# One row as a tile of its own, first in the queue; first weights right behind the memory tokens; small rows on GpSimd's queue

## The chip, the core and the metric

The kernel runs on one core of a Trainium2 chip. The core has TensorE (PE in the profile: matrix products and transposes), VectorE (DVE), ScalarE (ACT), GpSimd (POOL) and SyncE (SP, which only issues transfers here), and 16 DMA engines that serve the transfers that any engine issues. The metric is the device time of one execution in microseconds, the median of several runs.

## The reference

Two layers of a decoder trunk: a norm, one wide projection that feeds four token mixers, an output projection, and a feed-forward block. The fourth mixer attends into 256 memory tokens, and the start of the kernel, where the change lies, prepares it:

```python
def rmsnorm(x, g):
    y = x * lax.rsqrt(jnp.mean(x * x, axis=-1, keepdims=True) + EPS)
    return y * g

mem_n = rmsnorm(mem, mem_norm)                      # (256, 1024)
for l in range(2):
    h = rmsnorm(x, norm_mix[l])                     # (512, 1024)
    mk, mv = jnp.split(mem_n @ mem_w_kv[l], 2, axis=-1)   # 4 heads of 128 each
    mk = rmsnorm(mk.reshape(1, 256, 4, 128), mem_k_norm[l])
    ...
```

Everything is float32. `mem_w_kv[l]` is 1024 x 1024.

## The kernel before

**Products in three parts.** Every float32 product runs as three TensorE passes on split operands: a = a_hi + a_lo, and a·b is a_hi·b_hi + a_hi·b_lo + a_lo·b_hi. `mm3` (L267 to L272) issues the three; in the profile they are lines L270, L271, L272. Splitting an operand takes a ScalarE copy that rounds (w_hi, mt_hi, L97 being the line of the helper `A` that issues every ScalarE operation) and a VectorE subtraction (w_lo at L225, mt_lo at L394).

**Weights.** A `Chunk` (L212) loads 1 MB of weights into `w_raw` (two buffers) over SP's queue and splits it in two halves of 128 x 1024, each with one w_hi and one w_lo (three buffers each). A product needs the half of its rows; for the first weights of the memory, rows 0 to 511 (pieces 0 to 3 of the contraction) are the first half and 512 to 1023 the second.

**The start.** A few constants are set. TensorE runs 14 products on a constant (L143) as a warm-up. The memory tokens `mem_in` (1 MB, 256 x 1024) are loaded over SP's queue (L150), then eight small parameter tensors go into one tile `rows`, one parameter of 128 values per partition (L151 to L157): rows 0 to 39 (two norms and the memory's norm) over ScalarE's queue, rows 40 to 77 (conv_w, hgrn_lower_bounds, hgrn_out_norm, mem_q_norm, mem_k_norm) over SP's. One transpose turns `rows` (78 rows) into `prm`, 128 x 78 (L160, L161), so that each parameter is a column that ScalarE and VectorE can scale with; `g_mem(c)` is the memory norm's column for piece c of 8. GpSimd's queue carries five further loads (two gq_raw, two gk, the positions) and GpSimd makes two masks by a select (causal_bias, tri_f), from which VectorE derives `future` and `tri`.

**Memory tokens.** `mem_in_T` (L388) takes the 8 pieces c: two transposes into a PSUM tile `tr` (three buffers), an mt_hi and an mt_lo. Then two squares of the memory tokens with a sum (ScalarE, tile mem_sq) for the norm. `mem_kv(0)` (L433) has four weight chunks of 256 columns; for each, and for each half of the tokens, 24 products, and behind them copies (ku), squares (mk_sq), a norm and transposes. It runs in alternation with `first_h` (L404), which loads x in two transfers of 1 MB (`xin`), takes four squares of it (also into mem_sq), and transposes and splits it.

**Order.** A scheduler puts the instructions of each engine in one order at build time, by the order of the code and by priority (`high_priority` for the splits of weights); on the chip each engine works them off in that order, and waits on semaphores. A dependency of the kind `order` adds no semaphore, it only fixes two instructions' order on one engine. On SP the order is: memory tokens, five rows, first weights, x, x, second weights, third weights and so on. The changed kernel differs from this one in the order of TensorE's first 800 or so products of some 10,000, and in what goes with them on the other engines.

Of the kernel before, what the change touches and what calls it, by code (L numbers as in the profile page):

```python
# [21 lines left out]
P = 128  # L22
# [47 lines left out]
def hybrid_trunk(ctx: ExitStack, tc: tile.TileContext, x, mem, positions, norm_mix, w_in, conv_w,  # L70
# [38 lines left out]
    def tr_ps():  # L109
        return pat.tile([P, 512], F32, name="tr", bufs=TR_BUFS)  # L110
# [34 lines left out]
    rows = sp.tile([P, P], F32, name="rows")  # L145
    n_rows = 78
    warm = consts.tile([P, 1], F32, name="warm")
    A(warm, one, AF.Exp)
    mem_in = sp.tile([P, 2, D], F32, name="mem_in")
    nc.sync.dma_start(mem_in, mem[0].rearrange("(t p) d -> p t d", p=P))  # L150
    for lo, src in ((0, norm_mix.rearrange("l (c p) -> (l c) p", p=P)),  # L151
                    (16, norm_ffn.rearrange("l (c p) -> (l c) p", p=P)),
                    (32, mem_norm.rearrange("(c p) -> c p", p=P)),
                    (40, conv_w.rearrange("l w (c p) -> (l w c) p", p=P)),
                    (64, hgrn_lower_bounds.rearrange("l (c p) -> (l c) p", p=P)),
                    (72, hgrn_out_norm), (74, mem_q_norm), (76, mem_k_norm)):
        (nc.scalar if lo < 40 else nc.sync).dma_start(rows[lo:lo + src.shape[0], :], src)  # L157
    prm = consts.tile([P, n_rows], F32, name="prm")
    ps = tr_ps()
    pe.transpose(ps[:, :n_rows], rows[:n_rows, :], ident[:n_rows, :n_rows])  # L160
    A(prm, ps[:, :n_rows], AF.Copy)  # L161
# [7 lines left out]
    def g_mem(c):  # L169
        return prm[:, 32 + c:33 + c]  # L170
# [41 lines left out]
    class Chunk:  # L212
        def __init__(self, src, kt, n):
            self.kt, self.step = kt, min(kt, 1024 // n)
            raw = wpool.tile([P, 2048], F32, name="w_raw", bufs=RAW_BUFS)[:, :kt * n].rearrange("p (k n) -> p k n", n=n)
            nc.sync.dma_start(raw, src.rearrange("(k p) n -> p k n", p=P))
            self.parts = []
            for k in range(0, kt, self.step):
                e = min(kt, k + self.step)
                m = (e - k) * n  # L220
                hi, lo = (wpool.tile([P, 1024], F32R, name=nm, bufs=W_BUFS)[:, :m].rearrange("p (k n) -> p k n", n=n)
                          for nm in ("w_hi", "w_lo"))
                with tc.high_priority(offset=AHEAD):
                    A(hi, raw[:, k:e], AF.Copy)
                    dve.tensor_sub(lo, raw[:, k:e], f(hi))  # L225
                self.parts.append((range(k, e), hi, lo))

# [38 lines left out]

    def mm3(ps, a, b, first, last):  # L267
        ah, al = a
        bh, bl = b
        pe.matmul(ps, ah, bh, start=first, stop=False)  # L270
        pe.matmul(ps, ah, bl, start=False, stop=False)  # L271
        pe.matmul(ps, al, bh, start=False, stop=last)  # L272
# [115 lines left out]
    def mem_in_T():  # L388
        for c in range(KD):
            ps = tr_ps()  # L390
            for t in range(2):
                pe.transpose(ps[:, t * P:(t + 1) * P], mem_in[:, t, c * P:(c + 1) * P], ident)
            A(mt[0][:, c, :], ps[:, :MEM], AF.Copy, scale=g_mem(c))
            dve.scalar_tensor_tensor(mt[1][:, c, :], ps[:, :MEM], g_mem(c), f(mt[0][:, c, :]),  # L394
                                     op0=OP.mult, op1=OP.subtract)
        for t in range(2):
            A(mem_sq, mem_in[:, t, :], AF.Square, scale=D ** -0.5, accum_out=mem_ss[:, t:t + 1])
        rstd_into(mem_r, mem_ss, small, 2)
        dve.tensor_copy(mem_r4.rearrange("p (a b) -> p a b", b=2), mem_r[:, :, None].to_broadcast([P, 2, 2]))
        dve.tensor_mul(mem_r2, mem_r4, mem_r4)  # L400

# [31 lines left out]
    def mem_kv(l):  # L433
        kv = sp.tile([P, 4, 2, 2, MEM], F32R, name="kv", bufs=1)
        for q in range(2):
            w = wchunk(mem_w_kv[l][:, q * 256:(q + 1) * 256], KD, 256)
# [38 lines left out]
    mem_in_T()  # L475
# [19 lines left out]
    A(e0, e0, AF.Exp)  # L495
    A(e1, e1, AF.Exp)
# [634 lines left out]
```

## Time and profile before

| | us |
|---|---|
| median of 3 runs (2047.14 to 2047.64) | 2047.41 |
| the profiled execution | 2046.88 |
| its span, first to last instruction | 2044.9 |
| TensorE busy | 2032.3 |
| VectorE busy | 1274.7 |
| ScalarE busy | 1022.0 |
| TensorE's first product with w_lo | 14.03 |
| TensorE's first product of the second weights with w_lo | 22.16 |

The mean granted TensorE clock is 0.999 of full speed. Times within the execution count from the start of its span. In a row of a timeline, the first number is the start, the second the time busy; "out<-in" names the tiles; "x3" says that three instructions are drawn together; brackets give the idle time before it and what ended it. PEld is TensorE's weight load, SPq and ACTq are the parts of SP and ScalarE that issue transfers. In the list of queues, q1 is SP's, q10 ScalarE's, q0 GpSimd's.

### The profile page before, as it was taken

To read this page: it belongs to the slowest core of one execution; us is meant where nothing else is said; L and a number is where in the kernel's file an instruction comes from. 1 tells how busy PE (TensorE), PEld (TensorE's weight loads), DVE (VectorE), ACT (ScalarE), POOL (GpSimd) and SP (SyncE) were. 2 spreads that over 40 slices of the span, in tenths; PEclk is the share of its full clock that TensorE was granted. 3 is DMA by queue.
4 is the path that set the end of the run, shared out by engine and by line. 5 is a ranking of instruction groups with operands and counts; after the bars stand their busy time and mean duration, and the time that the engine had idled before them with its cause. 6 is when DMAs were issued, how large, how long until landed. Compare 5 with 4: busy or idle time off the path is not lost.

```text
span 2044.9 us, 26596 instructions
## 1 busy us (share of the span) xinstructions
PE 2032.3 (99%) x10348; PEld 1714.7 (84%) x10348; DVE 1274.7 (62%) x2519; ACT 1022.0 (50%) x1844; POOL 9.8 (0%) x33
## 2 busy tenths in 40 slices
PE   8999999999999999999999999999999999999999
PEld 8998988888888888888889898888888788888887
DVE  6779998547676544334457889953777654533442
ACT  7653655766665423223355466576766633322231
POOL 0000000000000000000000000000000000000000
PEclk9999999999999999999999999999999999999999
DMA  7623222223233232232243213322222423323222
GB/s 253 219 88 94 68 93 93 64 71 93 83 113 114 87 100 92 93 110 97 88 155 94 88 59 112 93 73 63 83 83 83 144 89 97 103 73 112 93 83 93
DMA packets 187709, 203.79 MB, mean 100 GB/s; under 512 B 4271, under 2 KB 176385, under 8 KB 187457
## 3 DMA queue, kind: packets, MB, share of 16 engines
q1 hardware_dynamic: 183296, 193.04, 29.7%
q10 hardware_dynamic: 4128, 8.93, 1.2%
q8 instruction: 81, 1.33, 0.3%
q14 instruction: 44, 0.35, 0.1%
q0 software_dynamic: 160, 0.13, 0.0%
HBM read 191.60 MB, written 10.49 MB: 99 GB/s over the span
## 4 chain that ended last, share of the span: by engine, by line
PE 98%; DMA 1%; ACT 1%; DVE 1%; issue 0%; SPq 0%; DVEq 0%
PE mm L270 30%; PE mm L271 29%; PE mm L272 29%; PE tr L726 1%; PE tr L720 1%; PE at L697 1%; PE at L696 1%; PE at L272 1%; PE at L270 1%; PE at L271 1%; DMA w_raw<-in_mem_w_kv_dram 1%; PE at L974 0%; PE at L948 0%; PE tr L664 0%; PE tr L765 0%; PE tr L631 0%
## 5 line engine op out<-in xcount | busy, mean ns | idle before, releaser
L270 PE MATMUL mm<-h_hi,w_hi 128*128 128x512 f32 x1664 | 652.0, 393 | 1.0 <-DVE fg L1075 0.4
L225 DVE TENSOR_TENSOR w_lo<-w_raw,w_hi 128x1024 fp32r<-128x1024 f32 (+1 forms) x346 | 419.7, 1214 | 372.3 <-ACT w_hi L97 371.9
L271 PE MATMUL mm<-h_lo,w_hi 128*128 128x512 f32 x1664 | 651.5, 392 | 0.0
L272 PE MATMUL mm<-h_hi,w_lo 128*128 128x512 f32 x1664 | 649.1, 391 | 0.0
L97 ACT ACTIVATE w_hi<-w_raw 128x1024 fp32r<-128x1024 f32 (+1 forms) x346 | 363.3, 1051 | 452.5 <-PE mm L271 406.1
L270 PEld LDWEIGHTS mm<-h_hi,w_hi 128*128 128x128 f32 x1664 | 312.7, 188 | 66.0 <-DVE fg L1075 1.2
L272 PEld LDWEIGHTS mm<-h_hi,w_lo 128*128 128x128 f32 x1664 | 312.6, 188 | 64.2 <-issue 0.2
L271 PEld LDWEIGHTS mm<-h_lo,w_hi 128*128 128x128 f32 x1664 | 312.8, 188 | 63.0 <-issue 1.0
L272 PE MATMUL mm<-w_hi,h_lo 128*128 128x256 f32 (+1 forms) x448 | 128.2, 286 | 0.0
L271 PE MATMUL mm<-w_lo,h_hi 128*128 128x256 f32 (+1 forms) x448 | 127.0, 284 | 0.0
L270 PE MATMUL mm<-w_hi,h_hi 128*128 128x256 f32 (+1 forms) x448 | 127.0, 285 | 0.0
L271 PE MATMUL mm<-a_lo,w_hi 128*128 128x512 f32 x272 | 106.3, 391 | 0.0
L270 PE MATMUL mm<-a_hi,w_hi 128*128 128x512 f32 x272 | 106.0, 390 | 0.0
L272 PE MATMUL mm<-a_hi,w_lo 128*128 128x512 f32 x272 | 105.7, 391 | 0.0
L270 PE MATMUL mm<-y_hi,w_hi 128*128 128x512 f32 x256 | 100.7, 395 | 1.2 <-ACT y_hi L97 1.2
L272 PE MATMUL mm<-y_hi,w_lo 128*128 128x512 f32 x256 | 100.4, 392 | 0.0
L271 PE MATMUL mm<-y_lo,w_hi 128*128 128x512 f32 x256 | 100.3, 392 | 0.0
L272 PEld LDWEIGHTS mm<-w_hi,h_lo 128*128 128x128 f32 x448 | 85.7, 191 | 1.4 <-issue 0.8
L270 PEld LDWEIGHTS mm<-w_hi,h_hi 128*128 128x128 f32 x448 | 85.3, 191 | 1.2 <-issue 0.8
L271 PEld LDWEIGHTS mm<-w_lo,h_hi 128*128 128x128 f32 x448 | 85.6, 191 | 0.6
L97 ACT ACTIVATE a_hi<-fg 128x512 fp32r<-128x512 f32 x44 | 27.8, 633 | 106.8 <-DVE fg L1080 106.8
L97 ACT ACTIVATE prob<-prob,small 128x128 f32<-128x128 f32 (+3 forms) x128 | 69.2, 555 | 15.2 <-DVE small L709 14.6
(370 smaller groups left out, 2958.1 us busy)
## 6 DMA issues: line engine op xcount, KB each, us to landing
w_raw<-in_w_in_dram SPq DMA_DIRECT2D x72, 1024.0 KB, 5.3
w_raw<-in_ffn_w_up_dram SPq DMA_DIRECT2D x44, 1024.0 KB, 5.1
w_raw<-in_w_lift_dram SPq DMA_DIRECT2D x32, 512.0 KB, 3.4
w_raw<-in_ffn_w_down_dram SPq DMA_DIRECT2D x16, 1024.0 KB, 5.4
w_raw<-in_mem_w_kv_dram SPq DMA_DIRECT2D x8, 1024.0 KB, 5.2
w_raw<-in_w_out_dram SPq DMA_DIRECT2D x8, 1024.0 KB, 5.3
w_raw<-in_ffn_w_down_dram SPq DMA_DIRECT2D x10, 512.0 KB, 3.4
kv<-kv ACTq DMA_DIRECT2D x8, 512.0 KB, 6.4
```

The source lines that it names most:

```text
L97: i = act.activation(dst, src, func, **kw)
L225: dve.tensor_sub(lo, raw[:, k:e], f(hi))
L270: pe.matmul(ps, ah, bh, start=first, stop=False)
L271: pe.matmul(ps, ah, bl, start=False, stop=False)
L272: pe.matmul(ps, al, bh, start=False, stop=last)
L696: pe.matmul(ps, q[:, hh, s], k[0][:, :n], start=True, stop=False)
L697: pe.matmul(ps, q[:, hh, s], k[1][:, :n], start=False, stop=True)
L720: pe.transpose(pp[:, (2 * e + i) * P:(2 * e + i + 1) * P], probs[2 * i + e][:, b * P:(b + 1) * P], ident)
L726: pe.matmul(pv[e * HD:(e + 1) * HD, :], vt[:, b, :], pt[:, b, e * 2 * P:(e + 1) * 2 * P], start=b == 0, stop=b == t)
```

## The change

The memory's norm row gets a tile of its own, `mem_row` (8 x 128), loaded by the first transfer of SP's queue, with a transpose and a column tile `mem_g` of its own; rows 32 to 39 of `rows` are set to zero instead. The five other small rows move from SP's queue to GpSimd's. The transpose of `rows` comes after the memory tokens' transposes. The first chunk of weights is made inside `mem_in_T`, ahead of piece 4: its load is next on SP behind the memory tokens; its first half is split ahead of the copies of pieces 4 to 7, its second half behind them. The squares of the memory tokens come after that. Behind the transposes of each piece stands a product on a constant, of which nothing is used. Two exponentials of the lower bounds come after the third w_hi or later.

```diff
     rows = sp.tile([P, P], F32, name="rows")
+    dve.memset(rows[32:40, :], 0.0)
...
+    mem_row = sp.tile([KD, P], F32, name="mem_row")
+    nc.sync.dma_start(mem_row, mem_norm.rearrange("(c p) -> c p", p=P))
     nc.sync.dma_start(mem_in, mem[0].rearrange("(t p) d -> p t d", p=P))
...
-                    (32, mem_norm.rearrange("(c p) -> c p", p=P)),
...
-        (nc.scalar if lo < 40 else nc.sync).dma_start(rows[lo:lo + src.shape[0], :], src)
+        (nc.scalar if lo < 40 else nc.gpsimd).dma_start(rows[lo:lo + src.shape[0], :], src)
+    mem_g = consts.tile([P, KD], F32, name="mem_g")
...
-    ps = tr_ps()
-    pe.transpose(ps[:, :n_rows], rows[:n_rows, :], ident[:n_rows, :n_rows])
-    A(prm, ps[:, :n_rows], AF.Copy)
+    def columns(dst, src, n, since=None):
+        ps = tr_ps()
+        i = pe.transpose(ps[:, :n], src[:n, :], ident[:n, :n])
+        if since is not None:
+            tc.add_manual_dep(i.ins, since.ins.name, order, reason="transposes first")
+        return A(dst, ps[:, :n], AF.Copy)
...
     class Chunk:
-        def __init__(self, src, kt, n):
+        def __init__(self, src, kt, n, held=False):
...
+            self.rest = self.make(raw)
+            for _ in range(1 if held else kt):
+                next(self.rest, None)
+
+        def make(self, raw):
+            kt, n = self.kt, raw.shape[2]
             for k in range(0, kt, self.step):
...
                 with tc.high_priority(offset=AHEAD):
-                    A(hi, raw[:, k:e], AF.Copy)
-                    dve.tensor_sub(lo, raw[:, k:e], f(hi))
+                    splits.append(A(hi, raw[:, k:e], AF.Copy))
+                    low = dve.tensor_sub(lo, raw[:, k:e], f(hi))
+                lowered.append(low)
                 self.parts.append((range(k, e), hi, lo))
+                yield
...
     def mm3(ps, a, b, first, last):
...
-        pe.matmul(ps, ah, bh, start=first, stop=False)
+        i = pe.matmul(ps, ah, bh, start=first, stop=False)
+        if turned:
+            tc.add_manual_dep(i.ins, turned.pop().ins.name, order, reason="transposes first")
...
     def mem_in_T():
+        first = []
+        columns(mem_g, mem_row, KD)
+        idle = at_ps()
+        keep = None
         for c in range(KD):
+            if c == 4:
+                first.append(Chunk(mem_w_kv[0][:, :256], KD, 256, True))
             ps = tr_ps()
             for t in range(2):
-                pe.transpose(ps[:, t * P:(t + 1) * P], mem_in[:, t, c * P:(c + 1) * P], ident)
...
+                i = pe.transpose(ps[:, t * P:(t + 1) * P], mem_in[:, t, c * P:(c + 1) * P], ident)
+                if t == 0 and keep is not None:
+                    tc.add_manual_dep(i.ins, keep.ins.name, order, reason="in between")
+            keep = pe.matmul(idle[:, :P], ones_d, ones_d, start=True, stop=True)
+            tc.add_manual_dep(keep.ins, i.ins.name, order, reason="in between")
+            copies.append(A(mt[0][:, c, :], ps[:, :MEM], AF.Copy, scale=g_mem(c)))
+            lows.append(dve.scalar_tensor_tensor(mt[1][:, c, :], ps[:, :MEM], g_mem(c), f(mt[0][:, c, :]),
+                                                 op0=OP.mult, op1=OP.subtract))
+            if c >= 4:
+                tc.add_manual_dep(copies[c].ins, splits[0].ins.name, order, reason="weights first")
+                tc.add_manual_dep(lows[c].ins, lowered[0].ins.name, order, reason="weights first")
+            if c == 3:
+                turned.append(i)
+        next(first[0].rest)
+        for c in range(4, KD):
+            tc.add_manual_dep(splits[1].ins, copies[c].ins.name, order, reason="copies first")
+            tc.add_manual_dep(lowered[1].ins, lows[c].ins.name, order, reason="copies first")
+        columns(prm, rows, n_rows, i)
         for t in range(2):
-            A(mem_sq, mem_in[:, t, :], AF.Square, scale=D ** -0.5, accum_out=mem_ss[:, t:t + 1])
+            square = A(mem_sq, mem_in[:, t, :], AF.Square, scale=D ** -0.5, accum_out=mem_ss[:, t:t + 1])
+            tc.add_manual_dep(square.ins, splits[1].ins.name, order, reason="copies first")
...
     def mem_kv(l):
...
-            w = wchunk(mem_w_kv[l][:, q * 256:(q + 1) * 256], KD, 256)
+            w = first_chunk.pop() if first_chunk else wchunk(mem_w_kv[l][:, q * 256:(q + 1) * 256], KD, 256)
...
-    mem_in_T()
+    first_chunk = mem_in_T()
     steps(mem_kv(0), first_h())
...
-    A(e0, e0, AF.Exp)
-    A(e1, e1, AF.Exp)
+    for e in (e0, e1):
+        i = A(e, e, AF.Exp)
+        tc.add_manual_dep(i.ins, splits[2].ins.name, order, reason="weights first")
```

More of the change, by code (lines that the diff above doesn't have):

```diff
@@ L169, in g_mem @@
     def g_mem(c):
-        return prm[:, 32 + c:33 + c]
+        return mem_g[:, c:c + 1]
     def g_conv(l, w, c):
@@ L212, in hybrid_trunk @@
     class Chunk:
-        def __init__(self, src, kt, n):
+        def __init__(self, src, kt, n, held=False):
             self.kt, self.step = kt, min(kt, 1024 // n)
             raw = wpool.tile([P, 2048], F32, name="w_raw", bufs=RAW_BUFS)[:, :kt * n].rearrange("p (k n) -> p k n", n=n)
-            nc.sync.dma_start(raw, src.rearrange("(k p) n -> p k n", p=P))
+            loads.append(nc.sync.dma_start(raw, src.rearrange("(k p) n -> p k n", p=P)))
             self.parts = []
+            self.rest = self.make(raw)
[3 more added lines that the diff above has]
+            kt, n = self.kt, raw.shape[2]
             for k in range(0, kt, self.step):
@@ L265, in tokens_wide @@
             k0 += w.kt
+    copies, lows, loads, splits, lowered, turned = [], [], [], [], [], []
     def mm3(ps, a, b, first, last):
@@ L400, in mem_in_T @@
         dve.tensor_mul(mem_r2, mem_r4, mem_r4)
+        return first
     norms = []
```

3 lines of the change are left out of this document (removed).

## The prediction

> **What bounds the kernel now.** First the page: the share of each engine.
>
> ```profile
> span 2044.9 us, 26596 instructions
> ...
> PE 2032.3 (99%) x10348; PEld 1714.7 (84%) x10348; DVE 1274.7 (62%) x2519; ACT 1022.0 (50%) x1844; POOL 9.8 (0%) x33
> ```
>
> TensorE idles 2044.9 - 2032.3 = 12.6 us in all. An edit that adds no matmul of weight can win no more than that, so the next view is the one that says where those 12.6 us lie: the chain of waits over the first 30 us, in order of time (start, length, what).
>
> ```profile
> 0.81 5.30 DMA mem_in<-in_mem_dram
> ...
> 6.40 0.41 SPq L216
> ...
> 7.98 11.79 DMA w_raw<-in_mem_w_kv_dram
> 19.79 1.07 ACT w_hi L97
> 20.88 1.24 DVE w_lo L225
> 22.16 0.39 PE mm L271
> ...
> 24.21 0.12 PE mm L270
> ```
>
> The memory tokens land at 0.81 + 5.30 = 6.11. The queue on SP then issues the first weights (6.40), two halves of x, and the second weights (7.98), which land at 19.77. ScalarE and VectorE split them, and TensorE goes on at 22.16. The last row shows the step from one product to the next, 0.12 us. Everything behind 22.16 is TensorE's own work, so what an edit of the start is worth is how far it moves the 22.16, less what it makes late behind it. Why the weights are issued only at 6.40 is in the waits of SP's queue:
>
> ```profile
> SPq L157 <- DMA mem_in<-in_mem_dram: 3.4, 1, 3.4
> ```
>
> A small row (L157) stands in front of the weights and waits 3.4 us for the memory tokens. How tight the stretches are, and the granted clock, by windows (busy time of each engine, granted clock, DMA share, GB/s):
>
> ```profile
> core 0: us, PE busy (x) PEld busy (x) DVE busy (x) ACT busy (x) POOL busy (x), PEclk, DMA share, GB/s
> 4.40:7.80 3.40, 1.70 (x15) 1.51 (x13) 0.37 (x3) 1.64 (x3) 0.67 (x3) 1.00 0.58 172
> 7.80:11.20 3.40, 2.23 (x13) 1.29 (x13) 2.48 (x13) 2.99 (x12) 0.00 (x0) 1.00 1.03 343
> 11.20:14.60 3.40, 1.57 (x9) 1.07 (x9) 2.48 (x10) 2.94 (x5) 0.00 (x0) 1.00 1.03 411
> 14.60:18.00 3.40, 3.40 (x19) 3.40 (x18) 2.75 (x12) 3.37 (x8) 0.00 (x0) 0.52 1.05 369
> 18.10:30.00 11.90, 11.36 (x95) 11.15 (x94) 6.98 (x14) 10.05 (x29) 0.00 (x0) 1.00 0.72 224
> 30.00:45.00 15.00, 15.00 (x130) 15.00 (x130) 12.87 (x31) 12.35 (x30) 0.00 (x0) 1.00 0.62 212
> 45.00:70.00 25.00, 24.90 (x204) 24.33 (x203) 19.80 (x72) 18.89 (x47) 0.52 (x1) 1.00 0.88 304
> ```
>
> Two things are to be seen. ScalarE works 10.05 of the 11.90 us from 18.10 to 30.00: it has 1.85 us to spare there and no more. And TensorE's clock was granted at half from 14.6 to 18.0, which cost nothing, since TensorE had to wait for the second weights anyway. The timelines give the unit prices (start, busy, engine, line, tiles, count):
>
> ```profile
> 1.12 4.98 PE L144 MATMUL tr<-ones_d 128*128 128x128 f32 x28 [1.12 <-DVE ones_d L118]
> 14.03 0.39 PE L271 MATMUL mm<-w_lo,mt_hi 128*128 128x256 f32 x1 [0.76 <-DVE w_lo L225]
> 15.35 0.41 PE L270 MATMUL mm<-w_hi,mt_hi 128*128 128x256 f32 x1
> 15.56 0.42 PE L271 MATMUL mm<-w_lo,mt_hi 128*128 128x256 f32 x1
> ```
>
> ```profile
> 11.66 2.00 ACT L97 ACTIVATE w_hi<-w_raw 128x1024 fp32r<-128x1024 f32 x2 [0.77 <-DMA w_raw<-in_mem_w_kv_dram]
> 13.57 1.18 ACT L97 ACTIVATE mt_hi<-tr,prm 128x256 fp32r<-128x256 f32 x3
> 14.64 1.06 ACT L97 ACTIVATE mem_sq<-xin 128x1024 f32<-128x1024 f32 x1
> 15.82 1.06 ACT L97 ACTIVATE mem_sq<-xin 128x1024 f32<-128x1024 f32 x1
> 25.33 1.06 ACT L97 ACTIVATE w_hi<-w_raw 128x1024 fp32r<-128x1024 f32 x1 [0.88 <-PE mm L272]
> ```
>
> One product at half clock steps 15.56 - 15.35 = 0.21. A w_hi costs ScalarE 2.00 - 1.06 = 0.94 in a row of them, a square 15.82 - 14.64 = 1.18, an mt_hi (1.18 - 0.47)/2 = 0.36.
>
> **The change part by part.** *The first transfer.* The 8-row load goes ahead of the memory tokens on SP. An 8-row issue takes
>
> ```profile
> 1.81 0.28 SPq L157 DMA_DIRECT2D rows<-n_hgrn_lower_bounds_dram  x1
> ```
>
> so about 0.3; the memory tokens are issued at 1.13 and land at 6.43 (+0.3). Its own landing, by the nearest row
>
> ```profile
> rows<-in_norm_mix_dram ACTq DMA_DIRECT2D x1, 8.0 KB, 3.1
> ```
>
> is near 4, before TensorE's warm-up ends (1.12 + 4.98 = 6.10); the little transpose and its copy are done near 6.6. Cost: nothing beyond the 0.3. If that row were served behind the 1 MB, the four first copies would end some 1.4 later and all that follows with them; this is in the upper end of the range.
>
> *The first weights right behind.* The five rows are gone from SP, so the weights are issued near 1.6 and follow the memory tokens without a gap. Three transfers of 1 MB back to back took 19.77 - 11.64 = 8.13, 2.71 each (11.64 is where the first weights' w_hi could start, row 11.66). So the first weights land at 6.43 + 2.71 = 9.14 and the second at 9.14 + 8.13 = 17.27, both 2.5 earlier. Bounds for 1 MB: 2.5 at the 417 GB/s quoted below, 3.1 at the 343 of the stretch 7.8 to 11.2; 2.71 is taken, because it comes from this very sequence. The bounds move the sum by -0.2 and +0.4.
>
> *The copies.* In the changed order ScalarE makes four mt_hi, then the first half of w_hi, then the other four mt_hi. VectorE's mt_lo sets the pace:
>
> ```profile
> 9.37 1.40 DVE L394 SCALAR_TENSOR_TENSOR mt_lo<-tr,prm,mt_hi 128x256 fp32r<-128x256 f32 x3
> ```
>
> 0.47 each, so the four are done by about 9.0, with the weights just landing. Then 1.09 for w_hi and 1.28 for w_lo, by the same steps as 19.79, 20.88 and 22.16: TensorE's stream begins at 9.14 + 2.37 = 11.5 instead of 14.03.
>
> *The eight added products.* Each is one 128-wide fp32 product, two instructions; the nearest are
>
> ```profile
> 33.74 0.60 PE L419 MATMUL tr<-diag,ones_h 128*128 128x128 f32 x4
> 34.10 0.36 PE L270 MATMUL mm<-w_hi,mt_hi 128*128 128x256 f32 x1
> ```
>
> four instructions in 34.10 - 33.74 = 0.36, so 0.18 a product. They stand between transposes, where TensorE waits for mt_lo's 0.47; uncovered they are 8 x 0.18 = 1.4, and even then they end before 11.5. I take 0. The memset on VectorE falls into its idle time before 6 us, and the two exponentials moved behind other work feed a branch that comes much later: 0.
>
> *What becomes late.* TensorE's instructions are in program order, and in the changed order the transposes of the eighth piece (c = 7) stand behind the first 21 products that need w_lo. They run at 11.5 + 21 x 0.12 = 14.0. ScalarE meanwhile idles, from the seventh mt_hi (about 11) to the eighth, about 14.45. And its order holds, behind that one, the second half of w_hi (14.8), the two squares of the memory tokens, which before ran from 6.13 in idle time, a few small ones (0.1 by estimate), one square of x, and only then the second weights' w_hi: 14.8 + 0.94 + 3 x 1.18 + 0.1 = 19.4. The second weights, landed at 17.27, wait 2.1 us for it. Against 19.79 that is -0.4, so TensorE goes on at 21.75 instead of 22.16. Nearly all of the 2.5 has been handed to ScalarE's queue.
>
> Three squares of x are still to do. Before, ScalarE went from 19.79 to the w_hi of row 25.33 in 5.54, 0.88 of it waiting: 4.66 of work. Now two squares (2.36) and five small ones (0.5 by the same estimate) stand between: 19.4 + 4.66 + 2.86 = 26.9, its w_lo at 28.0, ready at 29.3. TensorE needs it 60 products after going on, 21.75 + 7.2 = 28.95: a new stall of 0.35. Behind it lie 2.65 us of ScalarE's and 2.13 of VectorE's free time up to 45, and 0.10 of TensorE's from 45 to 70; small stalls there are bounded by 0 and 0.8, and 0.2 is taken, the end nearer to these rows.
>
> Sum: -0.4 + 0.35 + 0.2 = +0.15, say +0.2.
>
> *The five rows on GpSimd's queue.* They stand in front of the other loads there. The fourth gk issue now waits for conv_w's landing and the positions' issue for the lower bounds' landing; behind them on GpSimd stand the two selects, and behind these on VectorE `future` and `tri`, which in VectorE's order are ahead of the last mt_lo copies. Two windows of the transfers (queue: packets, MB, share), from 3.3 to 5.0 and from 5.0 to 7.0, tell what that queue does beside a large load, its first load having been issued long before:
>
> ```profile
> 1.34 0.71 POOL L182 DMA_DIRECT2D gq_raw<-in_dsa_q_norm_dram  x1 [0.34 <-issue]
> ```
>
> ```profile
> DMA packets 176, 0.71 MB, mean 417 GB/s; under 512 B 3, under 2 KB 3, under 8 KB 176
> ...
> q1 hardware_dynamic: 173, 0.71, 102.0%
> q10 hardware_dynamic: 3, 0.00, 0.1%
> ```
>
> ```profile
> q0 software_dynamic: 160, 0.13, 32.3%
> ```
>
> Nothing of GpSimd's loads (q0) moves while the memory tokens' packets run; all 160 packets follow at once afterwards. Now more transfers follow on SP without a gap. I take it that each queue gets its turn between whole transfers, so conv_w, first in its queue, lands near 7: cost 0. The other reading is a rival. [...]
>
> **The rivals.** *A. GpSimd's rows starve.* If q0 moves only when SP's queue is empty, conv_w comes behind the second weights, near 17.3 + 1 = 18.3. Then
>
> ```profile
> 3.47 0.54 POOL L188 DMA_DIRECT2D gk<-in_dsa_k_norm_dram  x1
> 4.00 0.52 POOL L330 DMA_DIRECT2D pos_i<-in_positions_dram  x1
> 4.53 0.30 POOL L132 TENSOR_SCALAR_AFFINE_SELECT causal_bias<-causal_bias 128x128 f32<-128x128 f32 x1
> ```
>
> one issue and a select (`future` at 19.2), another of each (`tri` at 20.0), the last mt_lo and w_lo at about 21.7, and the remaining 26 products of the first weights end at 24.8: +2.7 on 22.16, near 2050.3, up to 2052 with a clock at half in it. It decides once conv_w lands later than about 14. For it: the empty window. Against it: the windows show one large transfer, and not what happens between two.
>
> *B. The clock falls earlier.* The half clock came after the stretch in which TensorE was busy for 1.57 of 3.40, and not after those with 1.70 and 2.23. In the changed kernel the transposes and added products of 7.8 to 11.2 come to some 1.5 to 1.8, just there, and the stretch behind it now holds the 21 products that set ScalarE's queue: 21 x 0.21 instead of 2.5, up to +1.9, and +1.4 to +1.9 at the end: about 2049. A fall from 14.6 on stays free, as before. [...]
>
> *C. The gain arrives.* If ScalarE gets through its queue early (first weights sooner, squares overlapped), the second weights' landing binds: 17.27 + 2.37 = 19.65, -2.5, 2044.9. Against it is ScalarE's order, which is fixed; a part of it, -1, is likelier.
>
> *D. No effect:* the first weights still land near 11.6, because the rows' queues take turns in front of them. Then only the 0.3 and ScalarE's squares remain, +1, 2048.4.
>
> **How the numbers follow.** Forecast 0.45, A 0.13, B 0.23, C 0.13, D 0.06. The sum is made on the profiled execution (2046.88, its span 2044.9 and 1.98 around it), 0.5 below the median of the runs, 2047.41, to which +0.2 is added: 2047.6. The forecast's own range, by the bounds of the transfer and the small stalls, is 2046.8 to 2048.6. To hold 8 in 10 it reaches down to most of C and up to A: 2045.0 to 2050.8. Faster or slower by 0.2%, which is about what a measurement of this kernel can tell from no change, means 4.1 us. No case wins that: 0.03 for what I do not see. Slower by it needs A and B together, or a stall behind 30 us that no row shows: 0.13. Same: 0.84.
>
> **What would show it.** Right: the first product with w_lo near 11.5; the first weights landing near 9.1 and the second near 17.3; ScalarE idle from about 11 to 14.4, then busy without a gap to about 30; the second weights' w_hi at 19.4, 2 us behind their landing; TensorE going on near 21.75; a stall of 0.3 to 0.5 near 29. Wrong: w_hi of the second weights right at 17.3 (C); `future` or `tri` on VectorE behind 14 (A); a granted clock near 0.5 between 11 and 14.6 (B); the first w_hi after 11 (D); or a TensorE gap of over 1 us anywhere behind 30, which no step here has.

## The result, and the profile after

| | before | after |
|---|---|---|
| median of 5 runs, us | 2047.30 (2047.13 to 2047.64) | 2056.05 (2055.81 to 2058.49) |
| the profiled execution, us | 2046.88 | 2057.6 |
| its span, us | 2044.9 | 2055.9 |

The changed kernel is slower by 8.75 us: a ratio of 1.0046 [1.0034, 1.0057]. Forecast was 2047.6, in a range that ended at 2050.8. From the page of after:

```profile
span 2055.9 us, 26643 instructions
...
PE 2044.2 (99%) x10365; PEld 1719.2 (84%) x10365; DVE 1275.5 (62%) x2520; ACT 1021.6 (50%) x1845; POOL 12.3 (1%) x38
```

TensorE still idles only 2055.9 - 2044.2 = 11.7 us, no more than the 12.6 of before. So hardly any of the 11 us is a new wait: TensorE is *busy* 11.9 us longer (2044.2 - 2032.3), with 17 instructions more. Either the clock was lower for a while, or single products take longer.

To see where, the two traces are laid over each other from the end: the n-th TensorE instruction from the end in one against the same one in the other. It starts later in after by

| time in after, us | 25 | 70 | 200 | 700 | 1200 | 1630 | 1690 | 2000 | 2044 |
|---|---|---|---|---|---|---|---|---|---|
| later by, us | 2.48 | 3.10 | 3.07 | 6.72 | 6.70 | 8.64 | 10.27 | 10.33 | 10.33 |

There are two parts. The start, which the prediction is about, costs 3.1 in this execution. Then from 200 to 2000 us, where the diff touches nothing, 7.26 more trickle in, in both layers alike, and none of it in the feed-forward stretch from 700 to 1200. (The last 0.7 of the span's 11.0 comes behind TensorE's last products.)

**The trickle.** The groups of TensorE's products, each operand shape apart (busy us, mean ns of one). First before:

```profile
L270 PE MATMUL mm<-h_hi,w_hi 128*128 128x512 f32 x1664 | 652.0, 393 | 1.0 <-DVE fg L1075 0.4 <-DVE gate L530 0.3 <-DVE gate L549 0.3
L270 PE MATMUL mm<-y_hi,w_hi 128*128 128x512 f32 x256 | 100.7, 395 | 1.2 <-ACT y_hi L97 1.2
L270 PE MATMUL mm<-mg_hi,w_hi 128*128 128x512 f32 x128 | 49.4, 389 | 0.0
```

And after:

```profile
L287 PE MATMUL mm<-h_hi,w_hi 128*128 128x512 f32 x1664 | 651.9, 393 | 1.0 <-DVE fg L1117 0.4 <-DVE gate L572 0.3 <-DVE gate L591 0.3
L287 PE MATMUL mm<-y_hi,w_hi 128*128 128x512 f32 x256 | 101.9, 400 | 1.1 <-ACT y_hi L97 1.1
L287 PE MATMUL mm<-mg_hi,w_hi 128*128 128x512 f32 x128 | 50.1, 396 | 0.0
```

The same 512-wide product takes as long as before with h as the moving operand, and 5 to 7 ns more with y (a token mixer's output) or mg (the gated sum of the four). Consecutive products overlap (before, one on mg lasts 389 ns and the next starts 226.7 behind it), so the step from one to the next says more than the duration. One unbroken run of 192 products on mg, in TensorE's timeline before, first and last:

```profile
647.91 0.39 PE L270 MATMUL mm<-mg_hi,w_hi 128*128 128x512 f32 x1
...
691.21 0.39 PE L272 MATMUL mm<-mg_hi,w_lo 128*128 128x512 f32 x1
```

and after:

```profile
653.33 0.40 PE L287 MATMUL mm<-mg_hi,w_hi 128*128 128x512 f32 x1
...
697.89 0.40 PE L291 MATMUL mm<-mg_hi,w_lo 128*128 128x512 f32 x1
```

43.30 us against 44.56 in 191 steps: 226.7 against 233.3 ns, at the full granted clock in both (1.00 from 647.91 to 691.21 before and from 653.33 to 697.89 after). There are three times (256 + 128) = 1152 such products. With the traces laid over each other from 200 us on, the step behind a product on mg is 6.7 ns longer on the mean and behind one on y 5.3: 384 x 6.7 + 768 x 5.3 makes 6.6 of the 7.26. The rest is some 0.1 ns on each of the roughly 6,800 products on h and the other operands.

**The start.** The chain of waits of after, in order of time (start, length, what):

```profile
1.70 8.76 DMA w_raw<-in_mem_w_kv_dram
10.48 1.06 ACT w_hi L97
11.57 1.24 DVE w_lo L238
12.85 0.39 PE mm L290
...
17.38 0.47 ACT mt_hi L97
17.85 0.95 ACT w_hi L97
18.83 1.24 DVE w_lo L238
20.11 0.43 PE mm L290
```

The first weights land at 10.46, where the forecast had 9.14, and the 21 products behind 12.85 are slow. TensorE works at them until the eighth piece's transposes start at 16.96, for 4.11 us where the forecast had 2.5. Windows that follow the steps of the granted clock (it changes at 13.48, 16.89, 20.31 and 23.72) show why (busy us of PE, PEld, DVE, ACT, POOL, then the granted clock, DMA share, GB/s):

```profile
10.07:13.48 3.41, 2.05 (x14) 1.49 (x13) 2.11 (x4) 2.15 (x4) 0.00 (x0) 1.00 0.89 342
13.48:16.89 3.41, 3.41 (x18) 3.41 (x18) 0.77 (x4) 0.00 (x0) 0.00 (x0) 0.50 1.04 390
16.89:20.31 3.42, 1.49 (x10) 1.09 (x10) 1.97 (x5) 2.90 (x5) 0.00 (x0) 1.00 0.54 181
20.31:23.72 3.41, 3.41 (x17) 3.41 (x17) 0.43 (x2) 3.38 (x7) 0.00 (x0) 0.50 0.69 219
```

This is a clock fall as in rival B: the granted clock is 0.50 from 13.48 to 16.89, over the 21 products, and once more from 20.31.

### The profile page after: what moved, and what is told of

The parts are those of the page before. It is cut to its first block, busy times and chain, and to the rows that moved or that the text cites. A ratio compares the mean times of both kernels' runs of the same rounds, so it can differ in the third digit from the quotient of the medians.

```text
span 2055.9 us, 26643 instructions
## 1 busy us (share of the span) xinstructions
PE 2044.2 (99%) x10365; PEld 1719.2 (84%) x10365; DVE 1275.5 (62%) x2520; ACT 1021.6 (50%) x1845; POOL 12.3 (1%) x38
## 4 chain that ended last, share of the span: by engine, by line
PE 98%; ACT 1%; DVE 1%; DMA 0%; issue 0%; SPq 0%; DVEq 0%
PE mm L287 30%; PE mm L290 30%; PE mm L291 30%; PE tr L768 1%; PE tr L762 1%; PE at L739 1%; PE at L738 1%; PE at L291 1%; PE at L287 1%; PE at L290 1%; DMA w_raw<-in_mem_w_kv_dram 0%; PE at L990 0%; PE at L1016 0%; PE tr L706 0%; PE tr L807 0%; PE tr L673 0%
## 5 line engine op out<-in xcount | busy, mean ns | idle before, releaser
L97 ACT ACTIVATE prob<-prob,small 128x128 f32<-128x128 f32 (+3 forms) x128 | 69.2, 554 | 15.4 <-DVE small L751 14.8
```

What stands on the lines that cost most here:

```text
L97: i = act.activation(dst, src, func, **kw)
```

## The experiments on the slow products

**Theory.** `mem_g` is 8 float32 in each partition, 32 bytes, in `consts`, a pool that lives as long as the kernel. Everything placed behind it (h, w_raw, w_hi, w_lo) moves up by 32 bytes; y and mg, placed from the other end of the memory, stay. In the layout of the kernel before, y starts 105,216 bytes a partition from w_hi and mg 72,448, which is 411 x 256 and 283 x 256; after, both distances are 32 less. A w_hi buffer has 4096 bytes, so which buffer it is makes no difference. The theory: a product is slow when moving and stationary operand do not stand at some round distance. The rivals: it is the new order of instructions or transfers, or the address of one operand alone.

**e1_pad64** widens the tile, so that the shift is 64 bytes:

```diff
-    mem_g = consts.tile([P, KD], F32, name="mem_g")
+    mem_g = consts.tile([P, 2 * KD], F32, name="mem_g")[:, :KD]
```

> The changed kernel, with mem_g's tile 64 bytes wide in each partition instead of 32 (16 columns, 8 used). All instructions and their order stay; the tiles placed behind it move on by 32 more bytes, so that weights (w_hi, w_lo) and the mixers' operands (y, merged mg) stand in step modulo 64 again, as in the kernel before. Address theory: the 512-wide products of y and mg with weights, which cost 0.227 us each before and 0.232 to 0.234 after, go back to 0.227; of the changed kernel's 2056.05 us 7.3 go away: 2048.7 (2048.0 to 2050.5). Rival (the slow products come from the changed start or from the machine of that run): 2056 again, and the y and mg products at 0.232 to 0.234.

2055.30 against 2047.35 in the same batch, 1.0040 [1.0027, 1.0052]: still slow, mg's product at 394 ns. The round distance, if there is one, is not 64.

**e2_before32** is the kernel *before* with nothing but an unused tile of 32 bytes at that place:

```diff
+    pad = consts.tile([P, 8], F32, name="pad")
+    dve.memset(pad, 0.0)
```

> The kernel before, with nothing added but an unused tile of 32 bytes in each partition ahead of prm (and one memset of it on VectorE in idle time). Weights and h move by 32 bytes, y and mg do not. Address theory: +7.3 on 2047.3, so 2054.6, with TensorE going on at 22.16 as before and y and mg products at 0.232 to 0.234. Rival: 2047.3, products at 0.227.

2054.97, 1.0037 [1.0024, 1.0050]. A tile that nobody reads costs 7.6 us, nothing else being changed but its memset, and mg's product takes 396 ns as in after:

```profile
L272 PE MATMUL mm<-mg_hi,w_hi 128*128 128x512 f32 x128 | 50.1, 396 | 0.0
```

Behind 200 us its trace loses 7.29, after's 7.27. (TensorE went on with the second weights at 22.71, where 22.16 was expected: in this execution the clock was at half from 10.15 to 16.97.) That the change's new order makes the products slow is thereby ruled out.

**e3_before_right32** and **e4_after_right32** put the unused tile at the other end, so that y and mg move instead of w; in e3 the kernel is that of before, in e4 that of after:

```diff
+    edge = ctx.enter_context(tc.tile_pool(name="edge", bufs=1, side="right"))
+    dve.memset(edge.tile([P, 8], F32, name="pad"), 0.0)
```

> The kernel before, with an unused tile of 32 bytes at the other end of the memory: y and mg move by 32 bytes, weights and h do not. If what counts is the two operands' distance modulo 64: +7.3, 2054.6, y and mg products at 0.232 to 0.234. If what counts is that weights start at a multiple of 64 while y and mg do not: 2047.3, products at 0.227.

> The changed kernel, with the unused tile of 32 bytes at the other end: weights, h, y and mg are all at multiples of 64. If the distance modulo 64 counts: 2048.7 (2048.0 to 2050.5), y and mg products at 0.227. If only the place of the weights counts: 2056, products at 0.232 to 0.234.

e3: 2054.19, 1.0033 [1.0021, 1.0045], mg at 396 ns:

```profile
L272 PE MATMUL mm<-mg_hi,w_hi 128*128 128x512 f32 x128 | 50.1, 396 | 0.0
```

The weights stand where they stood and the products are slow, so the weights' address alone is not what counts. Nor do both operands have to stand at particular addresses: in after, h and w move up together by 32 bytes, and their product keeps its 393 ns. What is left is the distance. e4: 2057.99, 1.0050 [1.0037, 1.0062], mg at 394 ns. Its distances are off by 64 like e1's, and like e1 it missed its expectation and stayed slow.

**e5_start_pool** takes the shift away: `sp` is the pool of the start, which is given back.

```diff
-    mem_g = consts.tile([P, KD], F32, name="mem_g")
+    mem_g = sp.tile([P, KD], F32, name="mem_g")
```

> The changed kernel with mem_g's tile taken from the memory of the start instead of that of the constants: every instruction and its order stay, and weights, h, y and mg have the addresses of the kernel before. The runs so far: distances between y (or mg) and the weights that are 32 or 64 bytes off that of the kernel before cost the same 7.3 us. Address theory, with a period longer than 64 bytes: y and mg products at 0.227 again and about 2056 - 7.3 = 2048.7 (2048 to 2051, by the clock's falls at the start); all that is left, +1 to +3.5, is the start. Rival (the changed start slows the products behind it): 2055 to 2056.

2049.47 (2047.43 to 2055.31, 11 runs) against 2047.52, 1.0010 [1.0001, 1.0019]. In its trace TensorE is later than before by 3.81 at 200 us and by 3.87 at 2000: the trickle is gone. Its groups:

```profile
L287 PE MATMUL mm<-y_hi,w_hi 128*128 128x512 f32 x256 | 100.6, 394 | 1.2 <-ACT y_hi L97 1.2
L287 PE MATMUL mm<-mg_hi,w_hi 128*128 128x512 f32 x128 | 49.3, 389 | 0.0
```

**e6_before_less128** and **e7_before_less256** look for the period in the kernel before: small tiles leave `consts`, so that the distances grow by 128 or by 256.

```diff
-    mem_ss = small(2, name="mem_ss", bufs=1)
...
+    def own(n, name):
+        return sp.tile([P, 8], F32, name=name)[:, :n]
...
+    mem_ss = own(2, "mem_ss")
...
```

(In e6 the same for mem_r, mem_r2 and mem_r4; in e7 for xs too, `warm` goes to `sp`, and eps, half and one share a tile.)

> The kernel before, with four small tiles (mem_ss, mem_r, mem_r2, mem_r4, 32 bytes each in a partition) moved from the memory of the constants to that of the start, so that weights and h start 128 bytes earlier and y and mg stay. Before, the distances of y and of mg from the weights are multiples of 256 bytes. If the period is 128: products at 0.227, 2047.3. If it is 256 (or more): products of y and mg at 0.232 to 0.234, 2054.6.

> The same with five further small tiles taken together or moved (256 bytes in all). If the period is 128 or 256: y and mg products at 0.227, about 2047.3 (some instructions of the start change places). If it is 512 or more: 0.232 to 0.234, about 2054.6.

One run each. e6, 2053.72:

```profile
L270 PE MATMUL mm<-mg_hi,w_hi 128*128 128x512 f32 x128 | 50.1, 395 | 0.0
```

e7, 2046.45:

```profile
L269 PE MATMUL mm<-mg_hi,w_hi 128*128 128x512 f32 x128 | 49.3, 389 | 0.0
```

Slow with the distance off by 32, 64 and 128, fast with 0 and 256: the period is 256 bytes as far as these five values go (128 and 256 rest on one execution each). Why the chip does this no run here shows.

## The experiments on the start

With the addresses put right, e5 is still 1.95 above the kernel before. Its trace shows the first weights landing at 11.66, no earlier than before (11.64). What holds them up is seen in the transfers of after, from 8.75 to 10.25 (queue: packets, MB, share of 16 engines):

```profile
DMA packets 63, 0.14 MB, mean 96 GB/s; under 512 B 13, under 2 KB 23, under 8 KB 63
...
q0 software_dynamic: 20, 0.03, 91.0%
q1 hardware_dynamic: 43, 0.11, 20.7%
```

20 packets of GpSimd's queue take 0.91 x 16 x 1.5 / 20 = 1.1 us each, and the loads on SP's queue all but stop. The long packets belong to gq_raw and gk, one row broadcast to 128 partitions; in single packets of the trace, 14 of their 64 take 1.27 to 1.99 us. Before, these loads were first in their queue and ran from 5.2 to 5.9, at the end of the memory tokens' load and ahead of the weights; the same 64 packets then took 0.15 us on the mean and 0.52 at most. Now the five rows stand ahead of them, and they meet the end of the first weights and the start of x.

Single packets also show whom the stop hits. Of the 1024 packets of the first weights in after, 10 start behind 8.75, and one of these only at 9.89; in e5 the last 41 start one by one from 9.97 to 11.10. The landing comes 0.57 behind the start of the last packet in after (10.46) and 0.56 in e5 (11.66), so a few packets left behind are enough. The rest of the stop falls on x, and on all that follows it in SP's queue.

**e9_hold_gq** is e5 with the four loads held back until the fifth mt_hi is there, by a GpSimd copy of one element into each of their targets (their loop moves down in the code, behind the memory tokens' copies):

```diff
         a = sp.tile([P, HD], F32, name=f"gq_raw{l}")
+        pool.tensor_copy(a[0:1, 0:1], f(mt[0][0:1, 4, 0:1]))
...
         b = consts.tile([P, HD], F32, name=f"gk{l}")
+        pool.tensor_copy(b[0:1, 0:1], f(mt[0][0:1, 4, 0:1]))
```

> As e5_start_pool (2049.5 us), but the four loads of gq_raw and gk on GpSimd's queue are held back: each waits for a copy of one element of the fifth mt_hi, which comes behind the first weights' landing. The five small rows stay on GpSimd's queue. Theory: what made the first weights late (first w_hi at 10.5 to 11.7 instead of 9.15) are not the rows but gq_raw's packets, of which the first sixteen took 1.2 to 2.0 us each in the middle of the first weights' transfer. Then the first w_hi comes at 9.1 to 9.5 and the end about 1.5 us earlier: 2048 (2046.5 to 2049.5). Rival (the rows themselves do it, or a transfer of 1 MB in second place is that slow): first w_hi at 10.5 or later, 2049.5.

2047.40 (11 runs) against 2047.26, 1.0003 [0.9994, 1.0012]. The same stretch, 8.75 to 10.25:

```profile
DMA packets 219, 0.59 MB, mean 392 GB/s; under 512 B 29, under 2 KB 91, under 8 KB 219
...
q1 hardware_dynamic: 197, 0.59, 103.1%
q0 software_dynamic: 22, 0.00, 1.0%
```

The stop is gone, none of the 64 packets takes longer than 0.4 us, and so is the loss. The first w_hi came at 10.37, though, where 9.1 to 9.5 was expected: here too the last 20 packets of the first weights trail behind, from 9.2 to 9.69, with no long packet beside them (in e21 the last one starts at 9.09). What held these up stays open.

**e20_start_pool_again** and **e21_hold_gq_again** are the same two kernels once more, on one chip.

> e5_start_pool once more, on the same chip as the two others of this call. 2049.5 (2047.4 to 2051.5 for most runs), first w_hi between 10.4 and 11.7.

> e9_hold_gq once more. If GpSimd's broadcast loads make the first weights late: first w_hi 0.3 to 1.5 us ahead of that of e20, below 10.4, and a median 1 to 2 us below e20's, 2047.4. If not (the earlier difference was the chip's or the clock's): the same median as e20 within 0.5 us.

2048.72, 1.0008 [0.9999, 1.0016], and 2047.48, 1.0001 [0.9993, 1.0010]. Holding the loads is worth 1.2 here and 2.1 between e5 and e9; the intervals of the two overlap, but the direction came twice. In these two traces the first weights land alike (9.66 and 9.63), although in e20 13 packets are long, and the second ones at 19.87 and 18.17. When the first weights land thus varies by up to 2 us from run to run without the hold (9.66 in e20 to 11.66 in e5), and by 0.7 with it (9.63 to 10.34). What the hold moves every time is x: its last packet starts at 16.37 to 16.55 in the seven kernels that have after's order of loads (after, e1, e4, e5, e10, e12, e20), and at 14.16 to 14.75 in e9, e16 and e21. In e20 the third weights are late too: their last packet starts at 24.21 (22.36 in e21), their w_hi comes at 24.80 after ScalarE has idled for 0.87 (23.81 without a wait in e21), and TensorE has a stall of 0.84 at 30.52 that e21 has not. That this lateness is handed down from x to the third weights is argued and not shown.

e21 is the prediction's own chain without the two disturbances. ScalarE and TensorE in its timeline (start, busy, engine, line, tiles, count, idle before):

```profile
9.66 1.06 ACT L97 ACTIVATE w_hi<-w_raw 128x1024 fp32r<-128x1024 f32 x1
...
15.03 0.47 ACT L97 ACTIVATE mt_hi<-tr,mem_g 128x256 fp32r<-128x256 f32 x1 [3.22 <-PE tr L406]
15.40 1.05 ACT L97 ACTIVATE w_hi<-w_raw 128x1024 fp32r<-128x1024 f32 x1
...
19.95 1.99 ACT L97 ACTIVATE w_hi<-w_raw 128x1024 fp32r<-128x1024 f32 x2
```

```profile
12.03 0.38 PE L279 MATMUL mm<-w_lo,mt_hi 128*128 128x256 f32 x1 [0.76 <-DVE w_lo L227]
...
14.61 0.38 PE L406 MATMUL tr<-ident,mem_in 128*128 128x128 f32 x2
...
22.31 0.39 PE L279 MATMUL mm<-w_lo,mt_hi 128*128 128x256 f32 x1 [0.88 <-DVE w_lo L227]
```

**Other edits of the start.** *e8_rows_act* is e5 with the five rows on ScalarE's queue instead of GpSimd's.

```diff
-        (nc.scalar if lo < 40 else nc.gpsimd).dma_start(rows[lo:lo + src.shape[0], :], src)
+        nc.scalar.dma_start(rows[lo:lo + src.shape[0], :], src)
```

> As e5_start_pool, with the five small rows on ScalarE's queue instead of GpSimd's; the order of the instructions behind changes with it. If the rows on GpSimd's queue are what makes the first weights land at 10.4 to 11.6 instead of the forecast 9.1: the first w_hi at about 9.2 to 9.5, `future` back before 9, and 1 to 1.5 us off the start, 2047.5 (2046.5 to 2050). If GpSimd's old loads (gq, gk, positions) do it, or the load itself is that slow: first w_hi at 10.4 to 11.6 again.

2051.59, 1.0020 [1.0011, 1.0029]: 4 us slower than expected, and the first w_hi at 14.23, later than either case had it. The row shows why: ScalarE, which could issue the last of the rows only at 11.59, stood 9.58 us before it made mem_g, the first weights' landing being the last thing it waited for, and the transposes and copies came 4 us later. One thing it does tell: with no row ahead of them the broadcast loads ran from 5.48 to 9.80 and 17 of their 64 packets still took 0.8 to 1.94 us, and the first weights landed at 11.58. So it is not the rows' place in GpSimd's queue that makes these packets long.

```profile
11.88 0.18 ACT L97 ACTIVATE mem_g<-tr 128x8 f32<-128x8 f32 x1 [9.58 <-DMA w_raw<-in_mem_w_kv_dram]
```

*e10_c7_first* is e5 with all transposes ahead of the 21 products, *e12_no_keep* is e5 without the eight products on a constant.

```diff
-            if c == 3:
+            if c == KD - 1:
```

> As e5_start_pool, with the first product of the first weights ordered behind the transposes of the eighth piece (c = 7) instead of the fourth. Theory: ScalarE's wait of 3 to 5 us for the eighth piece, whose transposes stand behind 21 products (2.5 us, 4 with the clock at half), is what keeps the second weights' split late. Then the eighth mt_hi follows the seventh within 1 us, the second half of w_hi comes at about 13.5 to 14.5 instead of 18 to 19, and the end is 2 to 4 us earlier, though the scheduler puts the second weights' w_hi two operations further back: 2046.5 (2045 to 2049). Rival (the clock's half periods alone set the start): 2049.5.

```diff
-            keep = pe.matmul(idle[:, :P], ones_d, ones_d, start=True, stop=True)
-            tc.add_manual_dep(keep.ins, i.ins.name, order, reason="in between")
...
```

> As e5_start_pool, without the eight added products; the order behind changes a little (the second weights' w_hi comes ahead of a square). If the added products are hidden and useless: within 1 us of 2049.5, the clock's half periods at the same places. If they hold the clock up: half periods from 10 us on, as in the kernels without them, and 1 to 2 us slower. If they stand in the way: faster by their 1.4 us.

2054.41, 1.0035 [1.0022, 1.0047], and 2054.22, 1.0032 [1.0019, 1.0044]; neither settles what it was made for. In e10 the second half of w_hi comes at 14.19 as expected, 4.8 earlier than in e5, but the second weights' w_hi only at 20.88, behind squares and copies. And both lose some 5 us far from the edit, between 70 and 100 us, where the scheduler's new order lets TensorE reach the attention into the memory before its keys are there. TensorE's waits in e10:

```profile
PE at L287 <- DMA mk<-kv: 2.8, 1, 2.8
```

and the windows of e10 around it (PE, PEld, DVE, ACT, POOL, clock):

```profile
84.85:88.26 3.41, 1.74 (x16) 1.66 (x15) 1.88 (x4) 1.47 (x4) 0.00 (x0) 1.00 1.01 321
88.26:91.70 3.44, 2.28 (x13) 2.28 (x13) 0.23 (x2) 1.40 (x6) 0.66 (x3) 0.75 0.55 211
91.70:95.00 3.30, 3.30 (x23) 3.30 (x23) 1.01 (x4) 0.79 (x3) 0.00 (x0) 0.74 0.00 0
```

A wait of 2.8 us is followed by a stretch of half clock from 90.0 to 93.4, over which TensorE is busy; half of the 3.4, 1.7 us by estimate, is then lost to the clock. In e12 the wait is 1.8 us and the clock is at half from 88.98 to 95.8, which by the same estimate costs 3.4, more than the wait. At 25 us TensorE was 0.05 later than before in e12, and 0.12 in e21, which has the eight products: no price of theirs is seen, and with another order behind it e12 can't settle it. That they hold the clock up is not borne out: without them it stayed at full up to 88.98 in e12's trace, where half periods from 10 us on were expected for that case.

**Can the start be won?** *e13_second_next* is e9 with all transposes first (as in e10) and the second weights issued right behind the first, ahead of x:

```diff
+        first.insert(0, wchunk(mem_w_kv[0][:, 256:512], KD, 256))
```

> A version meant to be faster than both: e9 and e10 together, and the second weights' load issued right behind the first weights', ahead of x. If loads and ScalarE's order are what bound the start, TensorE has no wait for the second weights any more and goes on with them at 17.5 to 19 instead of 22.16: 2044.5 (2043 to 2046.5). Rival (x, its squares and its transposes, now later, become the bound): a TensorE gap of 1 us or more between 25 and 45, and 2047 or more.

2046.65 (2046.37 to 2048.12, 11 runs) against 2047.26, 0.9998 [0.9989, 1.0007]: the lowest median of all kernels with more than one run, and not a clear gain. In its trace TensorE is 3.24 ahead of the kernel before at 25 us, 1.41 at 30, 0.43 at 70 and 0.47 at 2000. The 3.2 are there, and handed back within 45 us, first of all to ScalarE at the third weights:

```profile
25.39 0.50 PE L276 MATMUL mm<-w_hi,mt_hi 128*128 128x256 f32 x2 [0.62 <-ACT w_hi L97]
26.65 0.38 PE L279 MATMUL mm<-w_lo,mt_hi 128*128 128x256 f32 x1 [0.76 <-DVE w_lo L227]
```

*e16_squares_later* is e9 with all transposes first and the squares of x moved behind the second weights' w_hi.

```diff
+        first_chunk.append(wchunk(mem_w_kv[0][:, 256:512], KD, 256))
...
-            A(mem_sq, xin[:, t, :], AF.Square, scale=D ** -0.5, accum_out=xs[:, t:t + 1])
+            i = A(mem_sq, xin[:, t, :], AF.Square, scale=D ** -0.5, accum_out=xs[:, t:t + 1])
+            tc.add_manual_dep(i.ins, splits[3].ins.name, order, reason="weights first")
```

> e9_hold_gq with the transposes of the eighth piece ahead of the first products and the four squares of x ordered behind both halves of the second weights' w_hi. Theory: ScalarE's queue (eighth piece, squares) is what holds the second weights' split 2 to 4 us behind their landing. Then that w_hi comes within 1 us of the landing (17 to 18.5) and TensorE goes on with the second weights at 19.5 to 21 instead of 22.16; but the squares come later and ScalarE has no slack up to 30, so that a part is handed back: 2046.3 (2045.3 to 2047.5). Rival (ku, ahead of the split in this order, waits for TensorE's first products): w_hi at 19 to 20.5, 2047.5.

2048.44, 1.0006 [0.9997, 1.0015]. The second weights landed at 18.34, their w_hi came at 19.45, since now a copy ku stood ahead of it that waits for TensorE. TensorE went on at 21.81, 0.35 before the kernel before, and the end was no better. In both orders tried ScalarE's queue took the gain back, each time at another place.

## Why the prediction was wrong

**The step that failed: "Everything behind 22.16 is TensorE's own work, so what an edit of the start is worth is how far it moves the 22.16, less what it makes late behind it."** Behind 22.16 it is TensorE's own work, and that work itself became dearer: the 1152 products on y and mg by 5.3 and 6.7 ns, 6.6 of the 7.3 us that come in behind 200 us and are gone in e5, out of 8.75 in all. The part-by-part list counted what the diff adds in instructions and transfers; it costed `mem_g` as a transpose and a copy and never as 32 bytes in a pool that lives to the end. e2, e3 and e5 show that those 32 bytes alone do it. None of the rivals had it, and "slower" at 0.13 was for waits. "A TensorE gap of over 1 us anywhere behind 30" would not have shown it either, as there is no gap.

**"The first weights land at 6.43 + 2.71 = 9.14": mis-sized.** Measured: 10.46 in after, 9.63 to 11.66 over the runs of e5, e9, e20 and e21. The weights were issued as early as foreseen. The rate was nearly right: in after 1014 of the 1024 packets were through by 8.79. The last one started at 9.89, and the landing came 0.57 behind it; the term, priced from transfers that ran alone, had nothing for packets that are left behind. GpSimd's broadcast loads, which now run in the same stretch, were not priced either. The section on the rows followed them as far as `future` and `tri`, that is, by whom GpSimd makes wait, and not by what they share the engines with.

**Rival B, at 0.23, came in its size, and not by its reason.** The fall was to follow a stretch from 7.8 to 11.2 with 1.5 to 1.8 us of TensorE's work; it followed the one from 10.07 to 13.48, with 2.05. B took 1.57 of 3.40 as too little and 1.70 as enough, from windows that cut across the clock's own steps. On windows that follow these steps, before has 1.62 from 4.48 to 7.90 and no fall, and 1.63 from 11.31 to 14.72 and a fall, so that line does not hold. The price was right: in after the 21 products took 4.11 us and in e21 14.61 - 12.03 = 2.58: +1.5, within the 1.4 to 1.9 given. With the weights' 10.48 - 9.66 = 0.82 later, the two make 2.35, and that is TensorE's distance at the second weights, 24.64 against 22.31. Not every run has it: in e9 and e20 the fall begins at 19.38 and 17.72, behind the 21 products, and in e21 there is none. With e5's 1.95 and e20's 1.25 the start costs 1.3 to 2.0 in the median, and the 7.3 on top make 8.6 to 9.3, around the 8.75 measured.

**The chain through ScalarE's queue was right.** e21, where neither disturbance struck, has each step later than forecast by what the weights landed later (9.66 for 9.14): the second half of w_hi at 15.40 for 14.8, the second weights' w_hi at 19.95 for 19.4, TensorE at 22.31 for 21.75. The second weights landed at 18.17 and waited 1.8 for ScalarE; 2.1 was the forecast. The sum, "+0.2", is near what the kernels with addresses and loads put right measure: +0.14 in e9, +0.01 in e21. That is luck in part. In e21 TensorE goes on 0.15 late, where -0.4 was forecast, and the stall of 0.35 foreseen near 29 does not come (e20 has one, 0.84 at 30.52): two misses that cancel.

**Rival A was wrong.** GpSimd's rows do not starve, and the reading taken, that each queue gets its turn between whole transfers, was wrong too. In after from 5.0 to 6.4, while the end of the memory tokens and the first weights fill the engines:

```profile
q1 hardware_dynamic: 311, 0.51, 96.6%
q0 software_dynamic: 59, 0.02, 4.9%
```

59 packets of GpSimd's queue move here beside 311 of SP's, and from 7.4 to 8.6, with the first weights under way, 85 beside 395. The empty window from 3.3 to 5.0 says nothing on turns: in all seventeen traces the first packet of GpSimd's queue comes 3.6 to 4.4 us behind its first issue (3.8 in before, 4.2 in after), and those of the held loads 3.5 to 4.2 us behind theirs in e9, e13, e16 and e21. Whether this delay needs a load beside it no run shows. `future` and `tri` ran at 13.50 and 14.03 in after, the latter just past the 14 that was to be A's sign, but GpSimd had done its part by 8.52, and no product waited for them.

**C and D.** C's condition never came in the changed kernel. In e13, which loads the second weights ahead of x, TensorE had more than C's 2.5 at 25 us, and the end was not clearly earlier: "nearly all of the 2.5 has been handed to ScalarE's queue" holds there too, only later in the kernel than written. D's landing was seen in e5 (11.66) and e8 (11.58); e8 had no row on GpSimd's queue, so it does not take the rows.

## What to carry to other kernels

When a diff adds a tile to a pool that lives as long as the kernel, price it in addresses too: compare the mean duration and the step of untouched products, operand by operand, before looking for a wait, and put what only the start needs into the start's pool. When a load is moved past others in a queue, follow those others to what they will now run beside. And a gain at the start is a gain only if the engine that feeds the next stage has the slack for it: read that from its busy share in the stretch behind (here ScalarE's 10.05 of 11.90), and look 60 us further for a wait that the new order makes.

## What the runs showed of the hardware

- A 512-wide product of split operands (those on mg) steps in 226.7 ns with moving and stationary operand 283 x 256 bytes apart in their partition (before), and in 233.3 with 32 less (after). Its duration is 389 ns at the distance of before (before, e5) and at 256 more (e7), and 394 to 396 with the distance off by 32, 64 or 128 (after, e1 to e4, e6).
- Packets of a broadcast of one 256-byte row, 2 KB each, took up to 1.99 us in after, where the ends of loads of 1 MB run beside them, against 0.15 on the mean and 0.52 at most for the same packets before, with 0.10 MB of SP's loads beside them from 5 to 7. Meanwhile, from 8.75 to 10.25, all transfers together moved 96 GB/s in after; with these packets held back (e9), 392. What makes them long stays open.
- The granted clock fell to half behind stretches in which TensorE had work. In before and after, each stretch at half clock within the span lasts 3.41 us (it starts at 14.72 in before, at 13.48 and 20.31 in after). After and e21 both first reach the full clock at 6.65, so windows of 3.41 us counted from there lie at the same times in both. From 10.07 to 13.48 PE is busy for 2.05 us in after, which the half clock follows. In e21 it is 2.65, which no half clock follows:

```profile
10.07:13.48 3.41, 2.65 (x21) 2.32 (x21) 2.60 (x5) 1.74 (x4) 2.34 (x7) 1.00 1.04 413
13.48:16.89 3.41, 2.25 (x18) 1.95 (x17) 0.89 (x2) 1.86 (x3) 1.01 (x2) 1.00 1.07 352
```

No fixed busy time parts the two cases. In the first 30 windows of 3.41 us of each of the seventeen traces, counted from where the clock first reaches full, none with 2.20 us of PE or more was followed by half clock; of the 26 at full clock with 2.05 or less, 20 were and 6 (1.56 to 1.84) were not.
